# Feed-forward weights of an encoder block: 4 KB slots through the whole kernel, and two block sums formed by an accumulating DMA

## The chip, the core and the metric

The kernel runs on one core of a Trainium2 chip. A core has TensorE (matmuls; the profile calls it PE, and its weight loads PEld), VectorE (DVE), ScalarE (ACT), GpSimd (POOL) and SyncE (SP), which here issues nearly all DMAs. The engines run their own instruction streams in order and wait for each other by semaphores; 16 DMA engines move the data. The metric is the device time of one execution in microseconds, the median of several runs.

## What is computed

One block of a streaming encoder on a sequence of 256 rows and a width of 2048, in float32. Attention makes up the first part. The change touches the second part, the feed-forward network, whose inner width is 5632 = 11 x 512:

```python
h2 = rmsnorm(x, ffn_norm_g[i])
x = x + (jax.nn.silu(h2 @ w_ffn_gate[i]) * (h2 @ w_ffn_up[i])) @ w_ffn_down[i]
return rmsnorm(x, final_norm_g)
```

## The kernel before

**Precision.** Each float32 operand is split into a high half, rounded to TensorE's fast float32 format, and a low half, the rest (`split`, lines 89 to 97): ScalarE casts the high half (L92), VectorE subtracts it from the source (L93). A product takes three matmuls (`mm3`, lines 174 to 178): high x high (L176), high x low weights (L177), low x high weights (L178). Weights arrive as float32 (a `raw` tile) and are split on the chip.

**The front** (`weights`, `project`, lines 134 to 613) makes up the first 945 us: input projections, two attentions, output projection. Its weights go through the pool `wp`: six `raw` slots, four `whi` and four `wlo` slots of 4 KB a partition each. After the last projection (`w_out`, L587) the sums of squares and transposes of the new x follow, with h2 = x transposed, scaled and split (`h2T`, L608). Then the front's pools are closed (L613), and the pools `fp` and `fq` of the feed-forward are laid over their memory; a tile there waits for whatever was in its place.

**The feed-forward** runs over 11 blocks of 512 inner columns (`hidden`, lines 675 to 720), in three parts of 4, 4 and 3 blocks; after each part follows its share of the down projection (lines 743 to 756). A block takes eight steps, each over a pair of 128-row slices of the weights, four tiles of 128x512: gate and up for either slice. Steps 1, 3, 5, 6 and 7 are *plain*: 8 products, 24 matmuls (`plain_weights`, L630). Steps 0, 2 and 4 (`SEVEN`) save one product of eight in the manner of Strassen and Winograd (`seven_weights`, L635; `seven_products`, L651): from the four weight tiles B11, B12, B21, B22 they form the sums T1 = B11 + B12 and T3 = B22 + B12 (L638, one operation on both), T2 = T1 + B22 (L639) and T4 = T2 + B21 (L640), on VectorE, then split B11, B21, B22 (into tiles `r`) and the four sums (into tiles `w`): 7 products, 21 matmuls. After step 4 the seven PSUM sums are combined (lines 689 to 695), at the block's end gate and up are added to that and go through silu (lines 709 to 719). The results of a block are transposed within the next one (`transposed`, L661, called by `between`).

`fp` has three `raw` slots of 8 KB, five `w` slots of 8 KB, two `r` slots of 6 KB: a plain step takes two `w` slots, a step of seven three `w` (one for the sums themselves, released early) and both `r`. The framework orders each engine's instructions at build time, by a simulated timeline; at run time each engine keeps that order.

Of the kernel before, what the change touches and what calls it, by code (L numbers as in the profile page):

```python
# [8 lines left out]
F32 = mybir.dt.float32  # L9
# [5 lines left out]
P = 128  # L15
# [23 lines left out]
def hybrid_block(ctx: ExitStack, tc: tile.TileContext, x, xT, gains, w_lat, w_kr, w_dqk, w_dv, w_g0, w_g1, b_gate,  # L39
# [4 lines left out]
    up = ctx.enter_context(tc.tile_pool(name="up", bufs=1))  # L44
    st = ctx.enter_context(tc.tile_pool(name="st", bufs=1))
    dram = ctx.enter_context(tc.tile_pool(name="dram", bufs=1, space=bass.MemoryType.DRAM))

    front = ExitStack()
    wp = front.enter_context(tc.tile_pool(name="wp", bufs=1))
    ap = front.enter_context(tc.tile_pool(name="ap", bufs=1))  # L50
    ps = front.enter_context(tc.tile_pool(name="ps", bufs=1, space=bass.MemoryType.PSUM))

# [81 lines left out]
    def weights(w, c, g0=0, ng=None, cut=None, alloc=None):  # L134

        m, n = w.shape[3:]
        cut = cut or m
        full = [P, 1024 // n, n] if n == 256 else [P, 2, 512]
        res = []
        for g in range(g0, g0 + (ng or w.shape[1])):  # L140
            raw = wp.tile([P, m, n], F32, tag="raw", name=nm("raw"), bufs=6, padded_shape=full)
            if alloc is None:
                for i in range(0, m, cut):
                    nc.sync.dma_start(out=raw[:, i:i + cut], in_=w[c, g, :, i:i + cut])
                whi = wp.tile([P, m, n], F32R, tag="whi", name=nm("whi"), bufs=4, padded_shape=full)
                wlo = wp.tile([P, m, n], F32R, tag="wlo", name=nm("wlo"), bufs=4, padded_shape=full)
            else:
                nc.sync.dma_start(out=raw, in_=w[c, g])
            for i in range(0, m, cut):
                if alloc is None:  # L150
                    hi, lo = whi[:, i:i + cut], wlo[:, i:i + cut]
                else:
                    hi, lo = alloc(F32R, (P, cut, n)), alloc(F32R, (P, cut, n))
                split(raw[:, i:i + cut], hi, lo)
                res += [(hi[:, j], lo[:, j]) for j in range(cut)]
        return res
# [315 lines left out]
    t1 = []  # L472
# [147 lines left out]
        return fq.tile(list(shape), F32, tag=f"q{role}", name=nm("q"), bufs=1)  # L620

    def load(src):
        raw = fp.tile([P, 4, 512], F32, tag="raw", name=nm("raw"), bufs=3)
        nc.sync.dma_start(out=raw, in_=src)
        return raw

    def wide(dt=F32R):
        return fp.tile([P, 4, 512], dt, tag="w", name=nm("w"), bufs=5)

    def plain_weights(src):  # L630
        raw, hi, lo = load(src), wide(), wide()
        split(raw, hi, lo)
        return [(hi[:, j], lo[:, j]) for j in range(4)]

    def seven_weights(src):  # L635

        raw, t = load(src), wide(F32)
        nc.vector.tensor_tensor(out=t[:, 0:2], in0=raw[:, 1::2], in1=raw[:, 0:1].broadcast_to([P, 2, 512]), op=ALU.add)  # L638
        nc.vector.tensor_tensor(out=t[:, 2], in0=t[:, 0], in1=raw[:, 3], op=ALU.add)  # L639
        nc.vector.tensor_tensor(out=t[:, 3], in0=t[:, 2], in1=raw[:, 2], op=ALU.add)  # L640
        rh, rl = (fp.tile([P, 3, 512], F32R, tag="r", name=nm("r"), bufs=2) for _ in range(2))
        split(raw[:, 1:4], rh, rl)
        th, tl = wide(), wide()
        split(t, th, tl)
        return [(rh[:, j], rl[:, j]) for j in range(3)], [(th[:, j], tl[:, j]) for j in range(4)]

    def part_of(a, h):
        hs = slice(h * P, (h + 1) * P)
# [1 line left out]

    def seven_products(q, pair, w, start, stop):  # L651

        (b11, b21, b22), (t1, t3, t2, t4) = w
        hi, lo = h2S[pair]
        s1, s3, s2, s4 = [(hi[:, j], lo[:, j]) for j in range(4)]
        a0, a1 = h2T[2 * pair], h2T[2 * pair + 1]
        for i, l, r in ((1, part_of(a0, 0), b11), (5, s1, t1), (7, s3, t3), (6, s2, t2),
                        (2, part_of(a1, 0), b21), (3, s4, b22), (4, part_of(a1, 1), t4)):
            mm3(q[i], l, r, start, stop and i in (1, 5, 6, 7))

    def transposed(f, alloc=lt, roles=(5, 6)):  # L661

# [12 lines left out]
    def hidden(c, between):  # L675

        pairs = len(h2T) // 2
        last = max(SEVEN) if SEVEN else None
        q, base = {}, None
        for p in range(pairs):  # L680
            if p == pairs - 2:
                between()
            if p in SEVEN:
                w = seven_weights(w_gu[c, p])
                if not q:
                    q = {i: bank(i) for i in (1, 5, 7, 6, 2, 3, 4)}
                seven_products(q, p, w, p == min(SEVEN), p == last)
                if p == last:
                    c1, v2, v3, d12, d22 = (sc() for _ in range(5))
                    nc.scalar.copy(c1, q[1])  # L690
                    nc.vector.tensor_tensor(out=v2, in0=c1, in1=q[6], op=ALU.add)
                    nc.vector.tensor_tensor(out=d12, in0=q[5], in1=v2, op=ALU.subtract)
                    nc.vector.tensor_tensor(out=v3, in0=q[7], in1=v2, op=ALU.add)
                    nc.vector.tensor_tensor(out=d22, in0=q[5], in1=v3, op=ALU.subtract)
                    base = ((c1, d12), (v3, d22))
                continue
            u0, g0_, g1_, u1 = plain_weights(w_gu[c, p])
            if 8 not in q:
                q[8] = bank(8)
            if not SEVEN and not p:  # L700
                q.update({i: bank(i) for i in (2, 3, 4)})
            for a, (wg, wu) in ((h2T[2 * p], (g0_, u0)), (h2T[2 * p + 1], (g1_, u1))):
                first_k = a is h2T[0]
                for h, (i, j) in enumerate(((2, 3), (4, 8))):
                    l = part_of(a, h)
                    end = a is h2T[-1]
                    mm3(q[i], l, wg, first_k, end)
                    mm3(q[j], l, wu, first_k or (j == 8 and SEVEN and p == 1 and a is h2T[2]), end)
        f = []
        for h, (i, j) in enumerate(((2, 3), (4, 8))):  # L710
            sg = nt()
            gate, up_ = q[i], q[j]
            if base:
                nc.vector.tensor_tensor(out=sg, in0=base[h][0], in1=gate, op=ALU.add)
                nc.vector.tensor_tensor(out=base[h][1], in0=base[h][1], in1=up_, op=ALU.add)
                gate, up_ = sg, base[h][1]
            nc.scalar.activation(out=sg, in_=gate, func=AF.Silu, scale=r2[:, h:h + 1])
            nc.vector.scalar_tensor_tensor(out=sg, in0=up_, scalar=r2[:, h:h + 1], in1=sg, op0=ALU.mult, op1=ALU.mult)  # L718
            f.append(sg)
        return f  # L720
# [42 lines left out]
        nc.gpsimd.tensor_scalar(out=rest[:, h:h + 1], in0=s3, scalar1=D * EPS, scalar2=None, op0=ALU.add)  # L763
    ws = []
    for m in range(a, b):
        raw = load(w_fd[3, m])
        for j in range(4):
            ws.append((lt(F32R, (P, 512)), lt(F32R, (P, 512))))
            split(raw[:, j], ws[-1][0], ws[-1][1])
    for h in range(2):  # L770
        hs = slice(h * P, (h + 1) * P)
        z, y = x2[3][h], lt(shape=(P, 512))
# [56 lines left out]
def _arrays(inputs):  # L829

    import numpy as np

    a = {n: np.asarray(v) for n, v in inputs.items()}
    a["xT"] = a["x"][0].T.reshape(D // P, P, S).transpose(1, 0, 2)
    a["gains"] = np.concatenate([a[n][0].reshape(-1, P).T for n in
                                 ("attn_norm_g", "ffn_norm_g", "q_norm_g", "kv_norm_g")], axis=1)
    w = a["w_in"][0]
    a["w_lat"], a["w_kr"] = _tiles(w[:, :1024], 512), _tiles(w[:, 1024:O_DQ], 320)
    a["w_dqk"], a["w_dv"] = _tiles(w[:, O_DQ:O_DV], 256), _tiles(w[:, O_DV:O_G], 512)
    a["w_g0"], a["w_g1"] = _tiles(w[:, O_G:O_G + D], 256), _tiles(w[:, O_G + D:], 512)  # L840
    w = a["w_uq"][0].reshape(QR, NH, QK)
    a["w_qn"] = _tiles(w[:, :, :NOPE].reshape(QR, -1), 256)
    a["w_qr"] = _tiles(w[:, :, NOPE:].reshape(QR, -1), 512)
    w = a["w_ukv"][0].reshape(KVR, NH, NOPE + VD)
    a["w_kn"] = _tiles(w[:, :, :NOPE].reshape(KVR, -1), 256)
    a["w_v"] = _tiles(w[:, :, NOPE:].reshape(KVR, -1), 256)
    for n, src, cols in (("w_mla", "w_mla_proj", 512), ("w_diff", "w_diff_proj", 512), ("w_out", "w_out", 512)):
        a[n] = _tiles(a[src][0], cols)

    wg, wu = (a[n][0].reshape(D // (2 * P), 2, P, NF, 512).transpose(3, 0, 1, 2, 4)  # L850
              for n in ("w_ffn_gate", "w_ffn_up"))
    a["w_gu"] = np.stack([wu[:, :, 0], wg[:, :, 0], wg[:, :, 1], wu[:, :, 1]], axis=3)
    a["w_fd"] = a["w_ffn_down"][0].reshape(NF, 4, P, 4, 512).transpose(3, 0, 2, 1, 4)
    a["consts"] = _constants()
    return [(n, np.ascontiguousarray(a[n])) for n in _INS]
# [16 lines left out]
```

## Time and profile before

| | |
|---|---|
| median of 3 runs | 1696.09 us (1696.07 to 1696.68) |
| the profiled execution | 1696.72 us, span 1694.9 us |
| TensorE busy | 1659.5 us, 98% |
| VectorE busy | 1146.8 us, 68% |
| ScalarE busy | 829.2 us, 49% |
| GpSimd busy | 27.5 us, 2% |
| mean DMA rate | 191 GB/s |

The span runs from the first to the last instruction of the profiled execution. Matmuls are pipelined and overlap in the records: a 512-column matmul is shown with 0.39 us, though the next one starts 0.23 us later. So the share of busy time says little about the distance to the peak; the waits of PE and PEld say where TensorE stood still. In a row, `out<-in` names tiles without numbers: `w`, `r` and `raw` are the slots told of above, `whi` and `wlo` those of the front, `q` the PSUM banks of the feed-forward, `L` long-lived tiles.

### The profile page before, as it was taken

The page shows a single profiled execution, that of the slowest core. Times are in us where ns is not written, and L with a number is a line of the kernel's source. Part 1 is how long each engine was busy: PE and PEld are TensorE (multiplying, and loading weights), DVE is VectorE, ACT ScalarE, POOL GpSimd, SP SyncE. Part 2 cuts the span into 40 slices and gives each one's busy share as a digit, 9 for nine tenths or more (in the row PEclk, how much of TensorE's full clock was granted, in tenths as well). Part 3 has the DMA queues.
Part 4 walks back from the last instruction along what each step waited for, and adds up shares of the span by engine and source line. Part 5 has one row for each costly group of instructions (what it writes and reads, how often), then busy time and mean ns, then how long its engine had stood idle before and what let it go on. Part 6 is the DMA issues. An engine that isn't in the chain of part 4 may idle for free.

```text
span 1694.9 us, 21463 instructions
## 1 busy us (share of the span) xinstructions
PE 1659.5 (98%) x8443; PEld 1405.4 (83%) x8443; DVE 1146.8 (68%) x1328; ACT 829.2 (49%) x998; POOL 27.5 (2%) x49
## 2 busy tenths in 40 slices
PE   8999999999999999999999899999999999999998
PEld 6888888888888999998888677787887777887776
DVE  7676666665545766665566688874688874588765
ACT  6455454544444665664444355543355553345532
POOL 0000000010000000000000000000000000000010
PEclk9999999999999999999999999999999999999999
DMA  9655455465665554456655455554555554555553
GB/s 324 217 174 174 174 175 180 146 205 201 217 207 190 175 175 166 160 191 223 233 201 199 142 180 199 199 199 174 183 201 189 197 199 174 200 198 197 185 195 118
DMA packets 80118, 323.61 MB, mean 191 GB/s; under 512 B 8848, under 2 KB 14992, under 8 KB 63120
## 3 DMA queue, kind: packets, MB, share of 16 engines
q1 hardware_dynamic: 79872, 322.21, 54.7%
q8 instruction: 66, 1.08, 0.3%
q14 instruction: 36, 0.29, 0.1%
q10 hardware_dynamic: 144, 0.02, 0.0%
HBM read 315.91 MB, written 6.29 MB: 190 GB/s over the span
## 4 chain that ended last, share of the span: by engine, by line
PE 88%; DVE 7%; issue 2%; ACT 2%; DMA 0%; SPq 0%; ACTq 0%; POOL 0%; POOLq 0%; DVEq 0%
PE mm L177 12%; PE mm L176 12%; PE mm L178 12%; PE q L177 11%; PE q L178 11%; PE q L176 10%; PE mm L201 9%; PE mm L202 5%; DVE w L93 3%; DVE r L93 2%; ACT w L92 2%; PE ps L178 1%; PE ps L177 1%; PE ps L176 1%; DVE n L718 1%
## 5 line engine op out<-in xcount | busy, mean ns | idle before, releaser
L93 DVE TENSOR_TENSOR wlo<-raw,whi 128x1024 fp32r<-128x1024 f32 (+3 forms) x320 | 381.8, 1193 | 266.2 <-ACT whi L92 260.0
L92 ACT CAST whi<-raw 128x1024 fp32r<-128x1024 f32 (+3 forms) x320 | 328.9, 1028 | 347.9 <-PE mm L178 221.6
L176 PE MATMUL mm<-whi,L 128*128 128x512 f32 (+2 forms) x1080 | 385.3, 359 | 5.4 <-ACT whi L92 5.4
L177 PE MATMUL mm<-wlo,L 128*128 128x512 f32 (+2 forms) x1080 | 386.0, 358 | 0.5 <-DVE wlo L93 0.5
L178 PE MATMUL mm<-whi,L 128*128 128x512 f32 (+2 forms) x1080 | 384.8, 357 | 0.0
L177 PE MATMUL q<-w,L 128*128 128x512 f32 x900 | 353.6, 393 | 11.6 <-DVE w L93 11.5
L178 PE MATMUL q<-w,L 128*128 128x512 f32 x900 | 351.0, 391 | 0.0
L176 PE MATMUL q<-w,L 128*128 128x512 f32 x900 | 308.8, 391 | 0.8 <-ACT w L92 0.7
L92 ACT CAST w<-raw 128x2048 fp32r<-128x2048 f32 x96 | 183.3, 1914 | 173.5 <-PE q L178 108.2
L93 DVE TENSOR_TENSOR w<-raw,w 128x2048 fp32r<-128x2048 f32 x96 | 219.6, 2288 | 57.5 <-PE q L177 38.0
L201 PE MATMUL mm<-L,whi 128*128 128x512 f32 x672 | 239.6, 398 | 0.6 <-DVE n L211 0.6
L176 PEld LDWEIGHTS mm<-whi,L 128*128 128x128 f32 x1080 | 204.1, 189 | 33.8 <-ACT whi L92 5.9
L177 PEld LDWEIGHTS mm<-wlo,L 128*128 128x128 f32 x1080 | 204.1, 189 | 28.9 <-DVE wlo L93 1.5
L178 PEld LDWEIGHTS mm<-whi,L 128*128 128x128 f32 x1080 | 204.0, 189 | 28.3
L177 PEld LDWEIGHTS q<-w,L 128*128 128x128 f32 x900 | 168.9, 188 | 54.8 <-DVE w L93 19.8
L176 PEld LDWEIGHTS q<-w,L 128*128 128x128 f32 x900 | 168.2, 188 | 36.1 <-ACT w L92 2.0
L178 PEld LDWEIGHTS q<-w,L 128*128 128x128 f32 x900 | 169.0, 188 | 34.0
L202 PE MATMUL mm<-L,wlo 128*128 128x256 f32 x672 | 189.2, 282 | 0.0
L201 PEld LDWEIGHTS mm<-L,whi 128*128 128x128 f32 x672 | 126.2, 188 | 28.7 <-DVE n L211 0.9
L202 PEld LDWEIGHTS mm<-L,wlo 128*128 128x128 f32 x672 | 127.0, 189 | 0.6
L92 ACT CAST w<-w 128x2048 fp32r<-128x2048 f32 x33 | 63.0, 1910 | 112.9 <-DVE w L640 98.6
L93 DVE TENSOR_TENSOR w<-w,w 128x2048 fp32r<-128x2048 f32 x33 | 75.6, 2292 | 59.7 <-ACT w L92 55.6
(190 smaller groups left out, 1364.8 us busy)
## 6 DMA issues: line engine op xcount, KB each, us to landing
raw<-in_w_gu_dram SPq DMA_DIRECT2D x88, 1024.0 KB, 4.7
raw<-in_w_fd_dram SPq DMA_DIRECT2D x44, 1024.0 KB, 4.7
raw<-in_w_dqk_dram SPq DMA_DIRECT2D x64, 512.0 KB, 4.0
raw<-in_w_g_dram SPq DMA_DIRECT2D x64, 512.0 KB, 3.3
raw<-in_w_diff_dram SPq DMA_DIRECT2D x32, 512.0 KB, 3.3
raw<-in_w_mla_dram SPq DMA_DIRECT2D x32, 512.0 KB, 4.2
raw<-in_w_out_dram SPq DMA_DIRECT2D x32, 512.0 KB, 3.9
raw<-in_w_dv_dram SPq DMA_DIRECT2D x30, 512.0 KB, 3.2
```

Source lines behind the costliest of these rows:

```text
L92: nc.scalar.copy(hi, src)
L93: nc.vector.tensor_tensor(out=lo, in0=src, in1=hi.bitcast(F32), op=ALU.subtract)
L176: nc.tensor.matmul(o, lhsT=l[0], rhs=r[0], start=start, stop=False)
L177: nc.tensor.matmul(o, lhsT=l[0], rhs=r[1], start=False, stop=False)
L178: nc.tensor.matmul(o, lhsT=l[1], rhs=r[0], start=False, stop=stop)
L201: nc.tensor.matmul(o[b], lhsT=ws[k][0][:, bs], rhs=a, start=k == 0, stop=False)
L202: nc.tensor.matmul(o[b][:, :S], lhsT=ws[k][1][:, bs], rhs=ah, start=False, stop=k == len(aT) - 1)
L718: nc.vector.scalar_tensor_tensor(out=sg, in0=up_, scalar=r2[:, h:h + 1], in1=sg, op0=ALU.mult, op1=ALU.mult)
```

## The change

The pool `wp` is opened for the whole kernel, and `whi` and `wlo` share one ring of eight 4 KB slots named `w`. The feed-forward takes its `raw` tiles (six of 4 KB) and the split weights of plain steps and of the sums T from the same rings. Each load and each split now covers two of the four tiles. The pool `fp` keeps five 4 KB slots `t`; a step of seven takes all five: the sums T1 and T3 (the tile `t13`, called T13 in the text), the sums T2 and T4 (`t24`), the high and low halves of B11 and B22, and one for both halves of B21. T13 is formed by two DMAs that GpSimd issues: a copy of B11 and B22 from DRAM, and one that adds B12 to both in the tile. VectorE still makes T2 and T4. B11, B22 and B21 are loaded by SP as well; B12 goes to the accumulating DMA only. In all steps of seven but a block's first, the products with B11, B22, B21 now come ahead of those with T. The weights lie in DRAM in the order B11, B22, B12, B21.

```diff
+    wp = ctx.enter_context(tc.tile_pool(name="wp", bufs=1))
     front = ExitStack()
-    wp = front.enter_context(tc.tile_pool(name="wp", bufs=1))
...
-                whi = wp.tile([P, m, n], F32R, tag="whi", name=nm("whi"), bufs=4, padded_shape=full)
-                wlo = wp.tile([P, m, n], F32R, tag="wlo", name=nm("wlo"), bufs=4, padded_shape=full)
+                whi = wp.tile([P, m, n], F32R, tag="w", name=nm("whi"), bufs=8, padded_shape=full)
+                wlo = wp.tile([P, m, n], F32R, tag="w", name=nm("wlo"), bufs=8, padded_shape=full)
...
     def load(src):
-        raw = fp.tile([P, 4, 512], F32, tag="raw", name=nm("raw"), bufs=3)
+        raw = wp.tile([P, 2, 512], F32, tag="raw", name=nm("raw"), bufs=6)
         nc.sync.dma_start(out=raw, in_=src)
         return raw
 
-    def wide(dt=F32R):
-        return fp.tile([P, 4, 512], dt, tag="w", name=nm("w"), bufs=5)
+    def two():
+        return wp.tile([P, 2, 512], F32R, tag="w", name=nm("w"), bufs=8)
+
+    def extra(dt=F32R):
+        return fp.tile([P, 2, 512], dt, tag="t", name=nm("t"), bufs=5)
+
+    def parts_of(src, alloc):
+        hi, lo = alloc(), alloc()
+        split(src, hi, lo)
+        return [(hi[:, j], lo[:, j]) for j in range(2)]
 
     def plain_weights(src):
-        raw, hi, lo = load(src), wide(), wide()
-        split(raw, hi, lo)
-        return [(hi[:, j], lo[:, j]) for j in range(4)]
+        return [w for m in (0, 2) for w in parts_of(load(src[:, m:m + 2]), two)]
 
     def seven_weights(src):
-        raw, t = load(src), wide(F32)
-        nc.vector.tensor_tensor(out=t[:, 0:2], in0=raw[:, 1::2], in1=raw[:, 0:1].broadcast_to([P, 2, 512]), op=ALU.add)
-        nc.vector.tensor_tensor(out=t[:, 2], in0=t[:, 0], in1=raw[:, 3], op=ALU.add)
-        nc.vector.tensor_tensor(out=t[:, 3], in0=t[:, 2], in1=raw[:, 2], op=ALU.add)
-        rh, rl = (fp.tile([P, 3, 512], F32R, tag="r", name=nm("r"), bufs=2) for _ in range(2))
-        split(raw[:, 1:4], rh, rl)
-        th, tl = wide(), wide()
-        split(t, th, tl)
-        return [(rh[:, j], rl[:, j]) for j in range(3)], [(th[:, j], tl[:, j]) for j in range(4)]
+        t13, t24 = extra(F32), extra(F32)
+        nc.gpsimd.dma_start(out=t13, in_=src[:, 0:2])
+        a = load(src[:, 0:2])
+        b = wp.tile([P, 2, 512], F32, tag="raw", name=nm("raw"), bufs=6)
+        nc.sync.dma_start(out=b[:, 1], in_=src[:, 3])
+        nc.gpsimd.dma_start(out=t13, in_=src[:, 2:3].broadcast_to([P, 2, 512]), accum_op=ALU.add)
+        nc.vector.tensor_tensor(out=t24[:, 0], in0=t13[:, 0], in1=a[:, 1], op=ALU.add)
+        nc.vector.tensor_tensor(out=t24[:, 1], in0=t24[:, 0], in1=b[:, 1], op=ALU.add)
+        w = {}
+        w[1], w[3] = parts_of(a, extra)
+        b21 = extra()
+        split(b[:, 1], b21[:, 0], b21[:, 1])
+        w[2] = b21[:, 0], b21[:, 1]
+        w[5], w[7] = parts_of(t13, two)
+        w[6], w[4] = parts_of(t24, two)
+        return w
...
-        for i, l, r in ((1, part_of(a0, 0), b11), (5, s1, t1), (7, s3, t3), (6, s2, t2),
-                        (2, part_of(a1, 0), b21), (3, s4, b22), (4, part_of(a1, 1), t4)):
-            mm3(q[i], l, r, start, stop and i in (1, 5, 6, 7))
+        ls = {1: part_of(a0, 0), 2: part_of(a1, 0), 3: s4, 4: part_of(a1, 1), 5: s1, 6: s2, 7: s3}
+        for i in (1, 5, 7, 6, 2, 3, 4) if start else (1, 3, 2, 5, 7, 6, 4):
+            mm3(q[i], ls[i], w[i], start, stop and i in (1, 5, 6, 7))
...
-            u0, g0_, g1_, u1 = plain_weights(w_gu[c, p])
+            g0_, u1, u0, g1_ = plain_weights(w_gu[c, p])
...
-        raw = load(w_fd[3, m])
         for j in range(4):
+            if j % 2 == 0:
+                raw = load(w_fd[3, m][:, j:j + 2])
...
-            split(raw[:, j], ws[-1][0], ws[-1][1])
+            split(raw[:, j % 2], ws[-1][0], ws[-1][1])
...
-    a["w_gu"] = np.stack([wu[:, :, 0], wg[:, :, 0], wg[:, :, 1], wu[:, :, 1]], axis=3)
+    a["w_gu"] = np.stack([wg[:, :, 0], wu[:, :, 1], wu[:, :, 0], wg[:, :, 1]], axis=3)
```

## Rows read from the trace of the kernel before

**Rows 1.** The page's busy time: us, share of the span, instructions of each engine.

```profile
PE 1659.5 (98%) x8443; PEld 1405.4 (83%) x8443; DVE 1146.8 (68%) x1328; ACT 829.2 (49%) x998; POOL 27.5 (2%) x49
```

**Rows 2.** Busy us (instructions) of each engine by stretch; then granted clock, DMA share, GB/s.

```profile
0.00:945.00 945.00, 938.45 (x5240) 818.75 (x5241) 598.10 (x860) 489.86 (x754) 16.50 (x35) 1.00 0.57 195
945.00:960.00 15.00, 10.02 (x33) 6.37 (x33) 12.54 (x18) 8.34 (x8) 1.07 (x3) 0.77 0.21 70
960.00:1142.00 182.00, 177.96 (x784) 143.61 (x783) 148.93 (x123) 91.29 (x63) 0.00 (x0) 1.00 0.54 193
1142.00:1226.00 84.00, 81.53 (x362) 66.79 (x361) 44.35 (x29) 29.16 (x17) 0.00 (x0) 1.00 0.51 182
```

**Rows 3.** Waits of the weight load, feed-forward: us in total, times, longest.

```profile
PEld q L177 <- DVE w L93: 19.8, 21, 1.7
PEld q L176 <- ACT r L92: 11.9, 11, 4.3
PEld q L176 <- ACT w L92: 2.0, 3, 1.1
```

**Rows 4.** Timeline, the passage: start us, us, engine, work [idle before <-releaser].

```profile
946.44 0.88 PE L601 MATMUL ps<-ident,L 128*128 128x128 f32 x6 [0.24 <-DVE L L593]
...
949.35 1.21 DVE L638 TENSOR_TENSOR w<-raw 128x1024 f32<-128x1024 f32 x1
...
951.36 1.65 PE L176 MATMUL q<-r,L 128*128 128x512 f32 x3 [4.04 <-ACT r L92]
...
954.30 0.63 PE L177 MATMUL q<-r,L 128*128 128x512 f32 x1
...
954.73 0.63 PE L178 MATMUL q<-r,L 128*128 128x512 f32 x1
```

**Rows 5.** Timeline between two blocks of gate and up.

```profile
1099.67 1.07 PE L176 MATMUL q<-w,L 128*128 128x512 f32 x4
1099.69 1.48 ACT L92 CAST r<-raw 128x1536 fp32r<-128x1536 f32 x1 [0.57 <-PE q L177]
...
1101.22 0.19 PEld L176 LDWEIGHTS q<-r,L 128*128 128x128 f32 x1 [0.90 <-ACT r L92]
...
1105.37 0.19 PEld L177 LDWEIGHTS q<-w,L 128*128 128x128 f32 x1 [0.82 <-DVE w L93]
```

**Rows 6.** Timeline, start of the first down projection.

```profile
1148.28 2.29 DVE L93 TENSOR_TENSOR w<-raw,w 128x2048 fp32r<-128x2048 f32 x1 [3.42 <-PE q L177]
...
1150.63 0.50 PE L177 MATMUL q<-w,L 128*128 128x512 f32 x1 [1.30 <-DVE w L93]
```

**Rows 7.** Groups by line and shape, columns as on the page: count, busy us, mean ns.

```profile
L93 DVE TENSOR_TENSOR wlo<-raw,whi 128x1024 fp32r<-128x1024 f32 x292 | 357.1, 1223 | 240.1 <-ACT whi L92 234.0 <-PE ps L514 3.5 <-DMA raw<-in_w_mla_dram 1.5
...
L92 ACT CAST whi<-raw 128x1024 fp32r<-128x1024 f32 x292 | 307.2, 1052 | 316.1 <-PE mm L178 205.4 <-PE mm L201 44.0 <-issue 32.2
...
L93 DVE TENSOR_TENSOR w<-raw,w 128x2048 fp32r<-128x2048 f32 x96 | 219.6, 2288 | 57.5 <-PE q L177 38.0 <-issue 12.9 <-PE q L178 3.5
...
L93 DVE TENSOR_TENSOR r<-raw,r 128x1536 fp32r<-128x1536 f32 x33 | 57.8, 1751 | 3.9 <-ACT r L92 3.9
...
L638 DVE TENSOR_TENSOR w<-raw 128x1024 f32<-128x1024 f32 x33 | 40.2, 1217 | 0.0
...
L93 DVE TENSOR_TENSOR L<-n,L 128x512 fp32r<-128x512 f32 x35 | 23.7, 683 | 2.2 <-ACT L L92 2.1
...
L640 DVE TENSOR_TENSOR w<-w,raw 128x512 f32<-128x512 f32 x33 | 22.8, 689 | 0.9
```

**Rows 8.** DMA issues: line, operation, count, KB each, median us from issue to landing.

```profile
raw<-in_w_gu_dram SPq DMA_DIRECT2D x88, 1024.0 KB, 4.7
...
raw<-in_w_dqk_dram SPq DMA_DIRECT2D x64, 512.0 KB, 4.0
raw<-in_w_g_dram SPq DMA_DIRECT2D x64, 512.0 KB, 3.3
```

**Rows 9.** Busy time as rows 2, a run of seven and plain steps.

```profile
1055.00:1080.00 25.00, 23.85 (x104) 18.77 (x104) 22.34 (x16) 13.03 (x9) 0.00 (x0) 1.00 0.60 212
```

More of the change, by code (lines that the diff above doesn't have):

```diff
@@ L651, in seven_products @@
     def seven_products(q, pair, w, start, stop):
-        (b11, b21, b22), (t1, t3, t2, t4) = w
         hi, lo = h2S[pair]
```

## Prediction

> **What bounds the kernel now.** I read the page's busy row first, then the busy time by stage, then what the weight loads of TensorE waited for, and last the timeline at the places where they waited. TensorE is busy for 98% of the span [rows 1]. By stage that is 938.45 of 945 us in the part ahead of the feed-forward, 177.96 of 182 in four blocks of gate and up, 81.53 of 84 in a stretch of the down projection, and only 10.02 of 15 in the passage at 945 to 960 us [rows 2]. The number of matmuls is not changed, so the ceiling of the gain is TensorE's waiting. In the feed-forward its weight loads waited 19.8 us for VectorE's low halves (21 times), 11.9 for the high halves of B11, B21 and B22 (11 times) and 2.0 for other high halves [rows 3]: 33.7 us. Such a wait partly overlaps the matmul before it, so this is an upper end.
>
> Where they are: **the passage.** The last transposes start at 946.44, and the first feed-forward matmul waits until 951.36, 4.04 us of it for the high half of B11, B21, B22. VectorE starts the first block sum only at 949.35, though the weights were loaded long before. The matmuls behind that wait follow each other at 0.43 us (954.30, 954.73), about half speed [rows 4]; the granted clock of the stretch is 0.77, against 1.00 in the others [rows 2], so some of it was granted at 1.2 instead of 2.4 GHz, behind the wait. In those 15 us there are 33 matmuls; at full speed 25 of them take 25 x 0.227 and the 8 transposes 8 x 0.15 (six in 0.88 [rows 4]), 6.9 us together, so 8.1 us are lost. **Between blocks.** Four matmuls take 1.07 us and one 0.39, so the cadence is (1.07 - 0.39)/3 = 0.227 us. At 1101.22 the weight load had waited 0.90 us for a cast that began at 1099.69, and at 1105.37 another 0.82 for a low half [rows 5]: 1.7 us. The same pair stands at eight of the eleven block starts, and rows 3 holds its sum. **Down projection.** At 1150.63 TensorE waits 1.30 us for a low half that VectorE began at 1148.28, when its slot came free [rows 6]; its weight load's wait is among the longest for a low half, 1.7 [rows 3]. There are six such waits, two at each of the three down projections: about 1.5 us each, 9 in all.
>
> **The change part by part.** A step of seven products has 21 matmuls, 21 x 0.227 = 4.8 us; a plain one 24, 5.4 us [rows 5].
>
> *VectorE, sums moved to the DMA.* A step of seven now costs it 1.217 + 2 x 0.689 + 1.751 + 2.288 = 6.63 us (the T split has the size of the plain one). After, the first sum is gone and the splits are three of 128x1024 and one of 128x512: 2 x 0.689 + 3 x 1.223 + 0.683 = 5.73 us. Over 33 steps that takes 30 us off VectorE. A plain step goes from one split of 2.288 to two of 1.223, + 0.16 us, 96 times: 15 us on again [rows 7]. Neither counts as time by itself, because TensorE sets the end. What counts is the run seven, plain, seven, plain, seven at a block's start, into which the evacuation of the block before falls (six operations of 128x512, about 0.7 us each, 4.2). VectorE needs 3 x 6.63 + 2 x 2.29 + 4.2 = 28.7 us there, TensorE 3 x 4.8 + 2 x 5.4 = 25.2: an excess of 3.5 us, which work done ahead hides in part. After: 3 x 5.73 + 2 x 2.45 + 4.2 = 26.3, an excess of 1.1. I take that a good two thirds of the waits between blocks go: 8 x 1.7 = 13.6, of which **-10 us** (bounds 0 and -13.6). ScalarE gets more instructions but has half its time free (91.29 of 182) [rows 2].
>
> *Slots of 4 KB kept through the kernel.* The feed-forward's weight slots no longer lie over memory of the front, so its first steps can be split while the last projection still runs. The tiles of the first sums lie in the memory of the attention pool, idle by then. The wait of 4.04 us goes, and with it the slow matmuls (nine, each 0.43 - 0.227 = 0.2) and the smaller waits behind them. **-7 us**; bounds 0 (the first step stays where the order puts it) and -8.1. In the down projection a half step can be prepared where a whole one waited for its slot, and eight slots are two steps where five were two and a half. I take **-6** of 9 (bounds 0 and -9). In the front, high and low halves now share one ring of eight instead of two of four; the count is the same. High halves that run ahead could hold the slots of low halves: I take 0, bounds -1 and +4, since TensorE is idle for only 6.6 us of its 945 [rows 2] and works with the same 4 KB tiles.
>
> *The accumulating DMA.* No row shows a DMA issued by GpSimd or one that accumulates. Per step of seven there are now 512 KB copied to T13, then 512 KB added to it, beside 768 KB on SP's queue in place of 1024. The pair is a chain: the addition waits for the copy, and the copy waits until the T13 before has been split, since each step takes all five slots of its ring. Let C be the time of copy plus addition. From below, two plain loads of 512 KB at 3.3 us: 6.6. From above, a copy at 4.7 and an addition at twice a 1 MB load, 9.4: 14.1. I take 4.0 (512 KB in the busiest group) + 4.7 (twice the bytes moved, as a 1 MB load), about 9 [rows 8].
>
> When does C show? Count from the end of the last plain step but one of a block, when slots for T13 of the next block's first step come free. A split takes 1.05 + 1.22 = 2.3 us [rows 7]. T13 of the third seven step is then split at 2.3 + 2 x (C + 2.3) = 6.9 + 2C. TensorE wants it after plain, seven, plain, seven, plain and nine matmuls: 3 x 5.4 + 2 x 4.8 + 2.0 = 27.8. So C may be 10.4, or about 8 if each split stands 2.4 us behind another operation on VectorE. With C = 9 I charge 0.2 us a block, **+2**, and another **+2** for waits at the smaller steps (the matmul behind a wait shows 0.50 instead of 0.39 [rows 6]). Who waits behind it: the sums T2 and T4 stand in VectorE's order and wait for the addition, and every plain split queued behind them waits too. GpSimd has next to nothing else (27.5 us in all [rows 1]).
>
> The Trainium skill (DMA: Bandwidth & Descriptors, Anatomy of one DMA) gives about 2.0 us plus bytes over 436 GB/s for a DMA issued from GpSimd: an estimate of 3.2 us for the copy. Collectives: The Full Stack (The bandwidth ceiling) says that an add in the DMA engines is slowed by its two source reads, which would make the addition 4.4 us, C 7.6, and the sum 4 us lower; no run here shows it yet.
>
> *Sum:* -10 - 7 - 6 + 2 + 2 = -19. The profiled execution took 1696.7 us with a span of 1694.9; the median is 1696.1, so 1.2 lies between span and median. 1694.9 - 19 + 1.2 = **1677**.
>
> **The rivals.** *The T13 chain sets the pace (slower).* Against: most loads land within 4.7 us. For: the DMA engines are 0.60 busy at 212 GB/s in the run of sevens and plains [rows 9], 5.3 MB in 25 us. Three steps add 3 x 0.79 MB moved and 3 x 0.52 MB read back, 9.2 MB; at 212/0.60 = 353 GB/s that is 26 us, so copy and addition compete with SP's loads for engines that are full, and C grows. At C = 12.5 the third step is late by 6.9 + 25 - 27.8 = 4.1 us, 11 blocks make 45, less the gains of 23: 1696 + 22 = 1718; at C = 14.1, 7.3 x 11 - 23 = +57: 1753. It decides above C = 11.5. The same page of the skill (Issuing engines are not separate DMA queues) says that DMAs of all issuing engines share the 16 engines: by that rule another queue adds no bandwidth, and this rival is the one it supports. Chance 0.36.
>
> *The gains are given back (no change).* Lateness of about 2 us a block eats the 23: 1695. Or the sums are ready, but the chain behind them (two adds, cast, subtraction, 2 x 0.69 + 1.05 + 1.22 = 3.7 us) becomes the wait at each block. Chance 0.09.
>
> *The passage stays.* The order of VectorE and ScalarE at 945 us puts the last h2 splits ahead of the first weights, as now [rows 4]. Then 7 us less gain: 1684, within the forecast's own range.
>
> **How the numbers follow.** Forecast 0.55 with a range of its own of 1660 (the 33.7 us of rows 3 and the slow clock's 2 all gone) to 1691; no change 0.09; slower 0.36, from 1700 to 1753. 1677 is the likeliest. For 8 in 10 the range must reach into the slow case: 1660 to 1735 leaves out few above (C over 13.3) and few below. A measurement of this kernel can tell about 0.2% from no change, 3.4 us. Faster 0.55, same 0.09, slower 0.36.
>
> **What would show it.** Right: no wait of 4 us ahead of the first q matmul and no granted clock under 1 there; the waits for low halves at block starts gone or below 0.5 us; VectorE's feed-forward time down by some 15 us; T13's copy plus addition within 10 us. Wrong: TensorE waiting for low halves of T13 or T24 at the second and third seven step, VectorE idle ahead of the T2 sum until a DMA on GpSimd's queue lands, DMA share near 1 in those stretches, or new waits in the front's low halves.

## The result and the profile after

The kernel got slower: 1778.58 us (median of four runs, 1775.4 to 1784.3) against 1696.38 beside it, a ratio of 1.0488 with a 95% interval of 1.0458 to 1.0518, 82 us more. Faster had been forecast, and the time lies 44 us above the range's upper end, on the side of the rival that the T13 chain sets the pace.

The page of the changed kernel: busy time of each engine as in [rows 1], and the shares of the chain of work that ended last, by engine; the last line is that chain in the kernel before.

```profile
PE 1687.8 (95%) x8443; PEld 1426.0 (80%) x8443; DVE 1123.7 (63%) x1457; ACT 841.2 (47%) x1158; POOL 86.2 (5%) x115
...
PE 74%; DMA 16%; issue 4%; DVE 4%; ACT 1%; SPq 0%; ACTq 0%; POOLq 0%; DVEq 0%; POOL 0%
```

```profile
PE 88%; DVE 7%; issue 2%; ACT 2%; DMA 0%; SPq 0%; ACTq 0%; POOL 0%; POOLq 0%; DVEq 0%
```

VectorE has 23 us less to do than in [rows 1] (15 had been worked out), as the sums were moved away, and the kernel is longer all the same. DMAs now hold 16% of the chain, some 280 us; before they had 0%.

What TensorE's weight loads waited for in the feed-forward, as [rows 3] (us in total, times, longest):

```profile
PEld q L176 <- ACT w L92: 49.5, 15, 7.1
PEld q L177 <- DVE w L93: 24.5, 10, 4.4
PEld q L176 <- ACT t L92: 8.9, 11, 2.1
PEld q L176 <- issue: 5.1, 1, 5.1
```

33.7 us of waits had become 88.0 (the last row is one wait, in the passage). The casts and subtractions that TensorE waits for waited in their turn. For VectorE and ScalarE the same view says (L649 is the first of the two sums that VectorE still makes, T2; "issue" is waiting for which the profile shows no releaser):

```profile
DVE t L649 <- DMA t<-in_w_gu_dram: 90.3, 19, 7.6
DVE t L649 <- issue: 72.8, 10, 9.4
...
ACT w L92 <- DMA t<-in_w_gu_dram: 157.1, 23, 11.2
```

The chain of waits in one stretch of a block, in order of time (start, us, what):

```profile
1099.90 1.14 DVE w L93
1101.04 0.28 issue
1101.33 5.16 DMA t<-in_w_gu_dram
1106.48 0.30 issue
1106.78 7.96 DMA t<-in_w_gu_dram
1114.84 1.05 ACT w L92
1115.92 1.24 DVE w L93
1117.15 0.28 issue
1117.44 4.71 DMA t<-in_w_gu_dram
1122.15 0.30 issue
1122.44 9.26 DMA t<-in_w_gu_dram
```

This is the turn of T13's slot, one and a half times: the split of one T13 ends, the copy for the next begins (5.16 us), then the addition (7.96), then cast and subtraction, and at once the next copy. Copy and addition take 13.4 us here and 14.3 in the next turn (over all 33 pairs the medians are 4.7 us for the copy and 9.2 for the addition), and nothing of a turn overlaps the next, because there is one slot. Matmuls appear nowhere in these lines.

What TensorE and GpSimd do meanwhile, from the timelines (columns as in [rows 4]):

```profile
1047.67 0.59 POOL L644 DMA_DIRECT2D t<-in_w_gu_dram  x1 [17.49 <-DVE w L93]
...
1101.33 0.59 POOL L644 DMA_DIRECT2D t<-in_w_gu_dram  x1 [16.98 <-DVE w L93]
...
1115.94 1.22 PE L176 MATMUL q<-w,L 128*128 128x512 f32 x2 [4.17 <-ACT w L92]
...
1117.38 0.63 PE L178 MATMUL q<-w,L 128*128 128x512 f32 x1
1117.81 0.63 PE L177 MATMUL q<-w,L 128*128 128x512 f32 x1
```

The two POOL rows are the same copy (for a block's second step of seven) in two blocks that follow each other: a block takes 53.7 us. TensorE waits 4.17 us for the cast at 1114.84, and the matmuls behind that wait follow each other at 0.43 us instead of 0.227, as in the passage before [rows 4]. Over that stretch, 1098 to 1137 us (columns as in [rows 2]), and in the one that answers to [rows 9]:

```profile
1098.00:1137.00 39.00, 32.76 (x128) 25.64 (x127) 23.36 (x27) 13.99 (x16) 4.13 (x5) 0.91 0.62 170
...
1055.00:1080.00 25.00, 21.19 (x81) 16.96 (x80) 12.75 (x14) 10.25 (x12) 2.36 (x3) 0.86 0.69 181
```

In the 25 us there are 81 matmuls, where [rows 9] has 104; the granted clock is 0.86 and the matmuls behind the wait come at half speed, so a long wait costs time at 1.2 GHz behind it as well, and VectorE is busy for half the time.

### The profile page after: what moved, and what is told of

Same layout as the page of the kernel before. It is cut to its first block, busy times and chain, and to the rows that moved or that the text cites. A ratio compares the mean times of both kernels' runs of the same rounds, so it can differ in the third digit from the quotient of the medians.

```text
span 1774.5 us, 22490 instructions
## 1 busy us (share of the span) xinstructions
PE 1687.8 (95%) x8443; PEld 1426.0 (80%) x8443; DVE 1123.7 (63%) x1457; ACT 841.2 (47%) x1158; POOL 86.2 (5%) x115
## 4 chain that ended last, share of the span: by engine, by line
PE 74%; DMA 16%; issue 4%; DVE 4%; ACT 1%; SPq 0%; ACTq 0%; POOLq 0%; DVEq 0%; POOL 0%
DMA t<-in_w_gu_dram 16%; PE mm L177 11%; PE mm L178 11%; PE mm L176 11%; PE mm L201 8%; PE q L176 8%; PE q L177 8%; PE q L178 7%; PE mm L202 4%; DVE w L93 2%; PE ps L178 1%; PE ps L177 1%; PE ps L176 1%; DMA raw<-in_w_dqk_dram 1%; ACT w L92 1%
## 5 line engine op out<-in xcount | busy, mean ns | idle before, releaser
L177 PE MATMUL q<-w,L 128*128 128x512 f32 x900 | 363.3, 405 | 20.8 <-DVE w L93 20.8
L176 PE MATMUL q<-w,L 128*128 128x512 f32 x900 | 332.3, 403 | 47.9 <-ACT w L92 43.2
L178 PE MATMUL q<-w,L 128*128 128x512 f32 x900 | 360.7, 403 | 0.0
L93 DVE TENSOR_TENSOR w<-raw,w 128x1024 fp32r<-128x1024 f32 x192 | 230.1, 1220 | 98.4 <-ACT w L92 98.4
L92 ACT CAST w<-raw 128x1024 fp32r<-128x1024 f32 x192 | 196.9, 1049 | 152.9 <-PE q L177 141.9
L176 PEld LDWEIGHTS q<-w,L 128*128 128x128 f32 x900 | 173.1, 194 | 89.9 <-ACT w L92 49.5
L177 PEld LDWEIGHTS q<-w,L 128*128 128x128 f32 x900 | 176.7, 196 | 62.2 <-DVE w L93 24.5
L178 PEld LDWEIGHTS q<-w,L 128*128 128x128 f32 x900 | 176.6, 196 | 37.4
L92 ACT CAST w<-t 128x1024 fp32r<-128x1024 f32 x66 | 69.1, 1048 | 198.8 <-DMA t<-in_w_gu_dram 157.1
L649 DVE TENSOR_TENSOR t<-t,raw 128x512 f32<-128x512 f32 x33 | 22.8, 692 | 168.1 <-DMA t<-in_w_gu_dram 90.3
```

Of the source, the lines that this page charges most:

```text
L92: nc.scalar.copy(hi, src)
L93: nc.vector.tensor_tensor(out=lo, in0=src, in1=hi.bitcast(F32), op=ALU.subtract)
L176: nc.tensor.matmul(o, lhsT=l[0], rhs=r[0], start=start, stop=False)
L177: nc.tensor.matmul(o, lhsT=l[0], rhs=r[1], start=False, stop=False)
L178: nc.tensor.matmul(o, lhsT=l[1], rhs=r[0], start=False, stop=stop)
L649: nc.vector.tensor_tensor(out=t24[:, 0], in0=t13[:, 0], in1=a[:, 1], op=ALU.add)
```

## Experiments

Theory A: the pair of DMAs for T13, on one slot, is longer than the order of work allows and sets the pace. Rival B: the small slots and finer splits cost the time. Rival C: the DMA engines are full. All times stand beside runs of the kernel before at 1696.5 to 1696.7 us.

**Slots alone.**

```diff
-        nc.gpsimd.dma_start(out=t13, in_=src[:, 0:2])
-        nc.sync.dma_start(out=b[:, 1], in_=src[:, 3])
-        nc.gpsimd.dma_start(out=t13, in_=src[:, 2:3].broadcast_to([P, 2, 512]), accum_op=ALU.add)
+        nc.sync.dma_start(out=b, in_=src[:, 2:4])
+        nc.vector.tensor_tensor(out=t13, in0=a, in1=b[:, 0:1].broadcast_to([P, 2, 512]), op=ALU.add)
```

> The changed kernel with its 4 KB slots, its smaller steps and its order of products, but T1 and T3 are again summed by VectorE (one operation of 128x1024, 1.22 us, 33 times) from B11, B22 and B12 loaded by SP; no DMA of GpSimd. Theory A (the chain of copy and addition for T13, some 13 us a step on one slot, sets the pace): the 82 us go and the gains of the passage and the down projection stay, 1683 to 1693 us. Rival B (the small slots and the finer splits cost the time): 1740 us or more. Rival C (the engines of the DMA are full): as A, since the extra traffic goes too.

Measured: 1666.89 us, ratio 0.9824 (0.9809 to 0.9838). That is 30 us below the kernel before and 16 below the lower end of what A expected. B falls. The waits of the weight load in the feed-forward are nearly gone; these are all rows of that view:

```profile
PEld ps L601 <- DVE L L593: 2.5, 2, 2.1
PEld q L176 <- PE q L178: 0.7, 1, 0.7
```

**Two slots for T13.**

```diff
-        t13, t24 = extra(F32), extra(F32)
+        t13 = fp.tile([P, 2, 512], F32, tag="t13", name=nm("t"), bufs=2)
+        t24 = extra(F32)
```

(and the ring `t` has four slots instead of five)

> The changed kernel with two slots for T13 instead of one (4 KB more a partition), all else kept. Theory A (chain on one slot): the next copy and addition run while the sums before are still being split, three chains of 13 us fit into a block of some 41 us of matmuls, so most of the waits go: 1685 to 1710 us. Rival C (DMA engines full, 16 engines shared by both queues): the same bytes move in less time, so it stays at 1750 to 1780 us. Rival B (small slots): stays at 1778 us.

Measured: 1664.48 us (1664.27 to 1664.48), ratio 0.9809 (0.9793 to 0.9826): 114 us less than the changed kernel, by one more slot, with the same bytes moved. It lies 21 us below the lower end of what A expected, and beats both kernels. C falls with that: the run of sevens and plain steps has the DMA engines 0.81 busy at 244 GB/s, and TensorE does 116 matmuls in the 25 us, without a wait. The stretch, then GpSimd's copies and additions (in this kernel at L645 and L649):

```profile
1055.00:1080.00 25.00, 25.00 (x116) 20.70 (x115) 21.50 (x28) 14.83 (x18) 2.94 (x3) 1.00 0.81 244
```

```profile
1038.74 0.59 POOL L645 DMA_DIRECT2D t<-in_w_gu_dram  x1 [5.35 <-DVE w L93]
1043.87 1.17 POOL L649 DMA_DIRECT2D t<-in_w_gu_dram  x1 [4.54 <-DMA t<-in_w_gu_dram]
1046.92 0.59 POOL L645 DMA_DIRECT2D t<-in_w_gu_dram  x1 [1.87 <-DVE w L93]
1057.64 1.18 POOL L649 DMA_DIRECT2D t<-in_w_gu_dram  x1 [10.13 <-DMA t<-in_w_gu_dram]
...
1081.19 0.59 POOL L645 DMA_DIRECT2D t<-in_w_gu_dram  x1 [5.07 <-DVE w L93]
```

At 1046.92 the next copy is issued 3 us behind the addition of the step before, while that is still under way (it landed after 10.9 us), because it has a slot of its own. 1038.74 and 1081.19 are the same copy in two blocks: 42.5 us, against 53.7 on one slot. The pair is no faster here (the addition at 1057.64 waited 10.13 us for its copy); it only runs ahead.

**No addition.** The second DMA is left out.

```diff
-        nc.gpsimd.dma_start(out=t13, in_=src[:, 2:3].broadcast_to([P, 2, 512]), accum_op=ALU.add)
```

> The changed kernel without the second DMA of each pair: T13 holds B11 and B22 alone, B12 is left out of the computation; all other instructions and waits are kept. Theory A: the chain is 5 us instead of 13, within what the order allows, so 1670 to 1690 us. Rival B: 1740 us or more. Rival C: the engines carry 0.5 MB less a step and read 0.5 MB less back, so some of the loss stays, 1700 to 1740 us.

Measured: 1667.18 us in one run, just below what A expected and far from B and C: with a chain of about 5 us, one slot is enough.

**The traffic without the wait.** T1 and T3 on VectorE, and the copy and addition into a tile `d13` that nothing reads.

```diff
+        d13 = fp.tile([P, 2, 512], F32, tag="d", name=nm("d"), bufs=1)
-        nc.gpsimd.dma_start(out=t13, in_=src[:, 0:2])
+        nc.gpsimd.dma_start(out=d13, in_=src[:, 0:2])
```

(the addition likewise goes to `d13`, and VectorE sums as in the run with the slots alone)

> VectorE forms T1 and T3 as in the run with the slots alone, and GpSimd issues the copy and the accumulating DMA of each step as well, into a tile of its own that nothing reads: the traffic without the wait. Theory A: within 6 us of the run with the slots alone. Rival C: the loads of SP slow down, 1730 us or more, most of the 82 us.

Measured: 1672.59 us in one run, 5.7 above the run with the slots alone, within A's 6 and far from C's 1730. But the traffic did not lie where the changed kernel has it. As nobody waits for `d13`, GpSimd ran ahead: 19 of the 33 pairs and one more copy ran between 385 and 661 us, in the front, the rest between 953 and 1152 us, and seven of the eleven blocks had none. So the 5.7 us are no price for the whole feed-forward. The first four blocks do tell something, with the idle traffic and with the slots alone (columns as in [rows 2]):

```profile
960.00:1142.00 182.00, 180.16 (x804) 147.43 (x803) 148.22 (x164) 95.01 (x107) 21.24 (x25) 1.00 0.87 268
```

```profile
960.00:1142.00 182.00, 182.00 (x819) 150.68 (x819) 149.67 (x165) 96.85 (x110) 0.00 (x0) 1.00 0.61 200
```

With the DMA engines 0.87 busy at 268 GB/s, TensorE does 15 matmuls fewer in four blocks, 15 x 0.227 = 3.4 us; for eleven blocks that would be some 9 us, an estimate. Contention is there, and far below the 82 us.

**A plain copy in place of the addition.**

```diff
-        nc.gpsimd.dma_start(out=t13, in_=src[:, 2:3].broadcast_to([P, 2, 512]), accum_op=ALU.add)
+        nc.gpsimd.dma_start(out=t13, in_=src[:, 2:3].broadcast_to([P, 2, 512]))
```

> The changed kernel, its one T13 slot kept, but the second DMA of each pair is a plain copy of B12 over the tile instead of an addition, so T13 holds B12 twice and the sums are left out; same bytes from DRAM, same chain of two. If the chain of two DMAs as such is too long (theory A1), the second takes some 5 us like the first, the pair 10 to 10.5 us instead of 13.3, and by 6.9 + 2C - 27.8 with some queueing the kernel comes to 1680 to 1710 us. If the addition's own time is what is too long (A2), the pair falls to 10 us or less and all waits go, 1665 to 1675 us. If the second DMA takes 8 us as a plain copy too (A3: the 2 KB pieces, not the addition), 1750 us or more.

Measured: 1717.19 us in one run, 7 us above A1's upper end and far from the times of A2 and A3. A turn of that kernel in the timeline:

```profile
1051.06 0.58 POOL L644 DMA_DIRECT2D t<-in_w_gu_dram  x1 [7.91 <-DVE w L93]
1055.81 0.71 POOL L648 DMA_DIRECT2D t<-in_w_gu_dram  x1 [4.17 <-DMA t<-in_w_gu_dram]
...
1062.51 1.06 ACT L92 CAST w<-t 128x1024 fp32r<-128x1024 f32 x1 [6.26 <-DMA t<-in_w_gu_dram]
```

From the copy's issue to the cast 11.45 us, against 13.5 and 14.4 in the changed kernel (1101.33 to 1114.84 above; 1117.44 to the next cast at 1131.80). So the addition costs 2 to 3 us more than a plain copy of the same bytes (medians over all 33: 9.2 and 6.8 from issue to landing), and a chain of two plain copies is too long already. What makes the addition longer is in part visible in GpSimd's DMA queue (packets, MB, share of the 16 engines' span), first the changed kernel, then this one:

```profile
q0 software_dynamic: 13728, 34.61, 8.9%
```

```profile
q0 software_dynamic: 9504, 34.61, 6.6%
```

The same bytes go in 128 packets more for each of the 33 additions, and they occupy all engines for 8.9% of 1774.5 us = 158 against 6.6% of 1715.4 = 113: 1.4 us more for each addition. The plain copy here has not the addition's packets, so whether the packets or the adding cost the time (A3) is open. These runs also give the price of C: from 11.45 to about 14 us the kernel grows from 1717 to 1779, 62/2.5 = 25 us for a microsecond, near the 2 x 11 = 22 of the prediction's formula. By 22 the 53 us between 1664.5 and 1717 are 2.4 us of C, so one slot is enough up to some 9 us: an estimate, as no run has a C between 5 and 11.

**The DMA alone, in the old slots.** In the kernel before:

```diff
-        raw, t = load(src), wide(F32)
-        nc.vector.tensor_tensor(out=t[:, 0:2], in0=raw[:, 1::2], in1=raw[:, 0:1].broadcast_to([P, 2, 512]), op=ALU.add)
+        t = wide(F32)
+        nc.gpsimd.dma_start(out=t[:, 0:2], in_=src[:, 1::2])
+        raw = fp.tile([P, 4, 512], F32, tag="raw", name=nm("raw"), bufs=3)
+        nc.sync.dma_start(out=raw[:, 1:4], in_=src[:, 1:4])
+        nc.gpsimd.dma_start(out=t[:, 0:2], in_=src[:, 0:1].broadcast_to([P, 2, 512]), accum_op=ALU.add)
```

> The kernel before with its 8 KB slots, but T1 and T3 formed by the copy and the accumulating DMA of GpSimd (SP loads B11, B21 and B22 only): the other part of the change alone. Theory A: the tile of the sums comes from the ring of five, is free no earlier than in the changed kernel, and the pair takes 12 us or more: 1740 to 1800 us. Rival (only together with the 4 KB slots is it slow): 1685 to 1700 us.

Measured: 1883.53 us in one run, 187 above the kernel before and 84 beyond the range expected. The direction is A's, the size is not. Two rows of its waits, of VectorE for the addition and of GpSimd for a slot:

```profile
DVE w L642 <- DMA w<-in_w_gu_dram: 218.8, 31, 10.1
```

```profile
POOL w L638 <- PE q L178: 396.1, 10, 114.1
```

31 of 33 sums waited for their DMA. The tile of 8 KB is free only when both later sums and one split of all four are done, and in ten cases its slot of the ring had held halves that TensorE was still reading, so the copy began only then (two of the ten, of 114 us each, span a down projection and cost little by themselves). How the 84 us divide between the two was not tried.

**Slots not kept through the kernel.** As the slots alone, but in the feed-forward's own pool (`raw` six, `w` eight, `t` five slots of 4 KB in `fp`).

```diff
-    wp = ctx.enter_context(tc.tile_pool(name="wp", bufs=1))
     front = ExitStack()
+    wp = front.enter_context(tc.tile_pool(name="wp", bufs=1))
...
-        raw = wp.tile([P, 2, 512], F32, tag="raw", name=nm("raw"), bufs=6)
+        raw = fp.tile([P, 2, 512], F32, tag="raw", name=nm("raw"), bufs=6)
```

> As the run with the slots alone (sums on VectorE), but the 4 KB slots of the feed-forward lie in its own pool over the front's memory, as before, instead of being kept through the kernel. By the prediction's term for the passage: 7 us above that run, 1672 to 1676 us. If keeping them is worth nothing: 1665 to 1669 us.

Measured: 1671.63 us, ratio 0.9856 (0.9841 to 0.9871), 4.7 above the run with slots kept. The wait of the passage is back:

```profile
952.41 1.22 PE L176 MATMUL q<-w,L 128*128 128x512 f32 x2 [4.75 <-ACT w L92]
```

So keeping the slots is worth 4.7 us. The other 25 are the small steps together with the new order of products and the shared rings; with sums on VectorE these were not tried one by one.

**A slot of its own for the sums, 8 KB slots.** In the kernel before, the tile of the sums has one slot of its own and the ring `w` four.

```diff
-        raw, t = load(src), wide(F32)
+        raw, t = load(src), fp.tile([P, 4, 512], F32, tag="t", name=nm("t"), bufs=1)
```

> The kernel before, 8 KB slots and whole splits, but the tile of the sums has a slot of its own and the ring w has four instead of five: same memory, no sum tile shifts the ring of halves. If the order of the ring causes the waits between blocks and in the down projection (theory R): 16 us or more less, 1672 to 1682 us. If it is the size of the splits (theory S): within 4 us of 1696.

Measured: 1693.87 us, ratio 0.9984 (0.9975 to 0.9994). Theory S's bound holds; the ring's order is worth 2.6 us, not 16.

**The same without any sums.** On top of that, the three operations that form the sums are left out and the raw tiles split in their place.

```diff
-        raw, t = load(src), fp.tile([P, 4, 512], F32, tag="t", name=nm("t"), bufs=1)
-        nc.vector.tensor_tensor(out=t[:, 0:2], in0=raw[:, 1::2], in1=raw[:, 0:1].broadcast_to([P, 2, 512]), op=ALU.add)
-        nc.vector.tensor_tensor(out=t[:, 2], in0=t[:, 0], in1=raw[:, 3], op=ALU.add)
-        nc.vector.tensor_tensor(out=t[:, 3], in0=t[:, 2], in1=raw[:, 2], op=ALU.add)
+        raw = load(src)
...
-        split(t, th, tl)
+        split(raw, th, tl)
```

> The kernel before with its 8 KB slots and whole splits (ring w of four, as in the run with an own slot for the sums, 1693.9 us), but VectorE forms no sums at all: the four raw tiles are split in their place, so the sums T are left out of the computation and the outputs are those of other products. VectorE has 2.6 us less in each of 33 steps of seven, 86 us in all, far more than the change takes off it. If the load of VectorE makes the waits between blocks (the prediction's step): they go, 1675 to 1682 us. If the size of the splits and the short lookahead make them: some stay, 1686 to 1694 us.

Measured: 1675.72 us, ratio 0.9878 (0.9849 to 0.9906), 18 below the run before it. Without the sums the waits between blocks go. That is not yet VectorE's load: the run also takes away the wait of the casts for the sums. The weight load's waits, first with the sums, then without:

```profile
PEld q L177 <- DVE w L93: 16.5, 15, 2.0
PEld q L176 <- ACT r L92: 11.4, 14, 4.3
```

```profile
PEld q L176 <- ACT r L92: 4.3, 1, 4.3
PEld q L177 <- DVE w L93: 3.5, 3, 2.0
```

What is left without sums is the passage (4.3) and, nearly all of it, the last down projection. The run with the slots alone speaks against the load by itself; this is its busy time:

```profile
PE 1648.2 (99%) x8443; PEld 1406.4 (84%) x8443; DVE 1158.8 (70%) x1490; ACT 844.7 (51%) x1158; POOL 26.8 (2%) x49
```

VectorE has all sums there and 12 us more to do than in [rows 1], and the waits are gone too.

**A ring of six.** The changed kernel with one number altered.

```diff
-        return fp.tile([P, 2, 512], dt, tag="t", name=nm("t"), bufs=5)
+        return fp.tile([P, 2, 512], dt, tag="t", name=nm("t"), bufs=6)
```

> The changed kernel with one number altered: the ring t has six 4 KB slots instead of five, so a step's T13 finds a slot that the step before does not hold; T13 has no ring of its own. Theory A (the pair of DMAs waits for the slot): as with two T13 slots, 1664 to 1675 us. If it took the separate ring: the sixth slot goes to another tile at times and 1690 us or more stay.

Measured: 1723.09 us (1714.9 to 1725.3), ratio 1.0146 (1.0116 to 1.0177). A's 1664 to 1675 missed; the other case named, that T13 needs a ring of its own, came true. The same 4 KB that bring 114 us as a second T13 slot bring 55 here. What GpSimd waited for ahead of its copies and additions, from 1000 us on:

```profile
POOL t L644 <- DVE w L93: 219.1, 4, 105.7
POOL t L648 <- DMA t<-in_w_gu_dram: 171.3, 26, 9.3
POOL t L644 <- PE q L178: 145.1, 20, 19.8
```

In 20 cases the copy waited for TensorE. Five tiles a step on a ring of six move each step's T13 to another slot; in these cases it was one that had held halves of B11, B21 or B22, which TensorE reads until the matmuls of an earlier step are done, where T13's own slot is free with its split. A gain was read off the number of slots where it hangs on whose slot it is.

**The old order of products, on two T13 slots.**

```diff
-        for i in (1, 5, 7, 6, 2, 3, 4) if start else (1, 3, 2, 5, 7, 6, 4):
+        for i in (1, 5, 7, 6, 2, 3, 4):
```

> As the run with two T13 slots, but all steps of seven keep the old order of products (1, 5, 7, 6, 2, 3, 4), so the products with T1 and T3 come second and third instead of fourth and fifth. With two slots T13 is there before its step begins: no change, 1663 to 1667 us. If the late place of the T products still covers part of the chain: 1670 us or more.

Measured: 1664.55 us, ratio 0.981 (0.9795 to 0.9824), the same as with the new order. Once T13 is early, the place of its products is worth nothing.

## Why the prediction was wrong, point by point

**The accumulating DMA: the step that failed.** The value of C, chosen as about 9, was the mis-sized term: it measured 13.4 and 14.3 us in the chain above, at the bound of 14.1. The copy was 4.0 in the sum and took 4.7 to 5.2; the addition was 4.7 and took 8.0 and 9.3. The row taken for it, a plain load of twice the bytes by SP, has neither the issue by GpSimd (1.18 us for the addition, 0.59 for the copy) nor the adding in the tile. Of the 4.5 us between 4.7 and the addition's median of 9.2, the plain copy in its place shows 2.1 as well and the adding brings 2.4; the causes behind these stay open. Between two bounds a factor of two apart, each microsecond of which was priced at 22 us a kernel, the middle was taken, and the forecast hung on it. Beside it, the Trainium skill's fit for a DMA issued from GpSimd (DMA: Bandwidth & Descriptors, Anatomy of one DMA) gives 3.2 us for 512 KB as an estimate, less than the 4.7 to 5.2 of the chain, where SP's loads ran on the same engines; its explanation of the cost of an add, in a collective's reduce step, by two source reads (Collectives: The Full Stack, The bandwidth ceiling) agrees with the runs in sign, the plain copy in the addition's place being 2 to 3 us shorter.

**The lateness behind it was too small as well.** With C = 13.9 the formula 6.9 + 2C - 27.8 gives 6.9 us a block, 76 us. The changed kernel lost 114 us against the same kernel with two slots, 10.4 a block. The prediction put the slow clock behind a new wait, 0.2 us a matmul, at nothing, though it had priced it in the passage. The mean granted clock fell from 0.999 over 1662.7 us (two slots) to 0.978 over 1774.5: 0.022 x 1774.5 - 0.001 x 1662.7 = 37 us, an estimate from above, as some of it fell into the waits themselves. Beside it the formula had the splits start as soon as T13 is there; the prediction itself named 8 instead of 10.4 as the limit with a queue on VectorE, and the plain second copy puts it near 9. In the rows, VectorE stands at L649 for the DMA, and what is queued behind it comes late too. How the 38 us beyond 76 divide between clock and queue was not tried. So the slower rival's upper end, 1753, was short by 26 us. Its chain on one slot, its place and its sign were right; its reason for a longer C was not, as the next point shows.

**DMA engines full: no.** The prediction scaled 0.60 at 212 GB/s to a share above 1. In the changed kernel the two stretches above have 0.62 and 0.69. With two T13 slots the stretch has 0.81 at 244 GB/s, and TensorE does not wait; the addition's median is 7.7 us there, against 9.2 on the emptier engines of the changed kernel: its length does not follow their share. The loads of 512 KB of gate and up weights by SP land in 5.5 us (median) against 4.7 with the slots alone. That agrees with the Trainium skill's rule that DMAs of all issuing engines share the 16 engines (DMA: Bandwidth & Descriptors, Issuing engines are not separate DMA queues).

**The passage, -7: within its bounds, then undone.** Keeping the slots is worth 4.7 us in the run without GpSimd's DMAs. In the changed kernel nothing of it is left:

```profile
945.11 1.18 POOL L648 DMA_DIRECT2D t<-in_w_gu_dram  x1 [4.66 <-DMA t<-in_w_gu_dram]
...
952.29 0.69 DVE L649 TENSOR_TENSOR t<-t,raw 128x512 f32<-128x512 f32 x1 [3.66 <-DMA t<-in_w_gu_dram]
952.90 0.48 DVE L96 SCALAR_TENSOR_TENSOR L<-ps,gT,L 128x256 fp32r<-128x256 f32 x1
...
956.00 0.76 PE L176 MATMUL q<-w,L 128*128 128x512 f32 x1 [4.70 <-DVE L L96]
```

The addition of the second step stands ahead of the h2 splits in VectorE's order; VectorE waits 3.66 us for it, and TensorE 4.70 for the split behind it. That a wait on an engine holds up what is queued behind it had been said of the plain splits; it was not applied to the passage.

**Between blocks, -10: the price was near, the cause not shown, and the remedy not the one that counted.** Without sums the old kernel takes 18 us less. But the small steps alone remove the waits with all sums left on VectorE, and there the prediction's own account, 3 x (1.22 + 2 x 0.69 + 3 x 1.22 + 0.68) + 2 x 2.45 + 4.2 = 29.9 us against TensorE's 25.2, has a larger excess than before, 4.7 us against 3.5. So the excess of VectorE alone does not make those waits; as far as the runs show, it takes the sums together with the steps and the order of the kernel before. In the kernel with small slots, moving T1 and T3 to the DMA is worth 1666.9 - 1664.5 = 2.4 us, and only with a second T13 slot. **Down projection, -6:** with the slots alone no wait of it is left, so all of the 9 us there were to be had. **Finer waits, +2:** not seen; with the slots alone the weight load waits 0.7 us in all for gate, up and down weights.

**The front, 0:** with two T13 slots TensorE's first transposes of the passage's last group come at 946.61 us, against 946.44 [rows 4]: 0.2 us.

## What to carry to other kernels

Before a sum goes to a chain of DMAs, work out the whole turn of its slot (free, copy, addition, the work that frees it again) and set it against the time between two uses; if the turn is longer, the tile needs a second slot of its own. More slots in a ring that tiles of different lives share are not that: the tile that must come early can inherit the slot of one that is held long. And where a duration that no row shows is multiplied many times in the sum, forecast by its bound, or say that the sign is open.

## What the runs showed of the hardware

An accumulating DMA of 512 KB into a tile, issued by GpSimd, took 8.0 and 9.3 us from issue to landing, a copy of the same size 4.7 to 5.2 and a plain copy in the addition's place 6.7 (1055.81 to 1062.51). The medians over 33 of each are 9.2 (5.3 to 11.8), 4.7 and 6.8. GpSimd's queue has 128 packets more for an addition than for the plain copy of the same bytes, and its packets take 1.4 us more of all 16 engines. GpSimd's own issue took 0.59 us for the copy, 0.71 for the copy of the same rows twice, 1.18 for the addition.
